# Weight parts made by one instruction a loaded chunk instead of two

## The chip, the cores and the metric

The kernel runs on one core of a Trainium2 chip. The metric is the device time of one execution in microseconds; the lower the better. Five engines work side by side, each through its own queue in order: TensorE (PE in the profile; its weight loads are listed as PEld) multiplies matrices, VectorE (DVE) and ScalarE (ACT) work elementwise, GpSimd (POOL) does the same more slowly, and SyncE (SP) issues the loads.

## The reference, cut to what matters

A decoder trunk of two layers with 256 tokens and a width of 2048, all in float32: layer 0 mixes tokens by the RWKV-7 recurrence, layer 1 by causal differential attention, and each is followed by a gated MLP with a causal depthwise convolution. Nearly all arithmetic is products of the activations with weights out of DRAM.

```python
def reference(x, ...):
    for i in range(DEPTH):                      # DEPTH = 2
        if i % 2 == 0:
            h, v_first = rwkv7_mix(x, ...)      # r, k, v = xr @ w_rkv[0], ...; scan over tokens; (y * g) @ w_o
        else:
            h = diff_attn_mix(x, ...)           # q, k, v = x @ w_qkv; softmax - lam * softmax; o @ w_o
        x = layer_norm(ALPHA * x + h, ...)
        x = layer_norm(ALPHA * x + conv_glu(x, ...), ...)   # (u * gelu(conv(g))) @ w_down, width 5504
    return x
```

## The kernel before

Activations lie with features on the partitions, in 16 tiles of 128 features ("k-tiles") by 256 tokens. A float32 product is made of products of two parts: an operand is split into `hi`, its rounding to the float32r type, and `lo`, the rest. For a weight block and one k-tile TensorE multiplies `hi` with both parts of the activations, which lie side by side (512 columns, line 225), and `lo` with the first part (256 columns, line 226). In the narrow form (lines 221 to 223) there are three matmuls of 256 columns in place of these two.

The weights' parts are made while the kernel runs, in `chunk`. A load (line 204) brings a chunk of up to `WCH = 4` k-tiles, 128 x 512 numbers, into a `raw` tile. Then, for each `HCH = 2` k-tiles, ScalarE makes `hi` by a cast (line 210), and VectorE makes `lo = raw - hi` (line 213). POOL takes over some of the subtractions: every third in the front, every fourth in the recurrence (`pool_every`), and those of the very first chunks. A `hi` or `lo` tile holds 128 x 256 numbers, a "half". Some chunks are shorter: two k-tiles for some pieces of the output projection of layer 0 and for two fifths of the pieces of `Ahead`, three at the end of each block of the MLP's second product, which has 43 k-tiles.

Tiles come from pools with a fixed number of buffers: `raw`, `hi` and `lo` have (3, 4, 4) in the first pool, which is there throughout (`PACE["w0"]`), and in those that single stages add; (6, 6, 6) in the one of the front (`PACE["vw"]`). Chunks take the open pools in turn. In the recurrence only the first pool is open. When the instructions are written, a scheduler orders them per engine by priority, by when a tile is free and by estimated durations; on the chip each engine's order is then fixed, and the waits between engines are by semaphores.

The stages, in order of time:

- the front (to about 160 us): `mix` makes the inputs of the six projections from the tokens and their shift, on VectorE and POOL, each split into its parts (lines 767, 191, 192), while the value projection and three small ones run (`lead`, `dense_pair`)
- the recurrence (to about 660 us): `pipeline` runs four steps side by side for groups of two feature tiles, `chain`, `lanes`, `front` and `products`, at set paces. `products` are the projections for k and r, in the narrow form; the others are many small matmuls with VectorE and ScalarE work between them. Towards the end `early` begins the output projection
- the rest of the output projection, the norm, and the first MLP. `Ahead` begins the first products behind a norm before the norm is known (lines 890 to 892)
- the two products of the first MLP (`glu`), the attention, the second MLP, the last norm. During the first MLP's second product a table of biases is written to DRAM and read back (`bias_table`, lines 590 and 593), in the queue of the weight loads

Of the kernel before, what the change touches and what calls it, by code (L numbers as in the profile page):

```python
# [32 lines left out]
HCH = 2  # L33
PACE = dict(chain=37.24, front=19.56, lanes=19.55, products=40.92, pool=4, pool0=3, chain0=0, front0=0,
            lanes0=0, early0=0, products0=0, wc='PVVA', ek='AA', ez='VA', ec='AVAA', ey='V', el='V', w0=(3, 4,
            4), lb=1, early=46.23, vw=(6, 6, 6), vp=2, ep='V', eg='A', lg=2, lr=2, la=4, ah=10, ao=12, ah0=0.05)
# [89 lines left out]
class Trunk:  # L126
    def __init__(self, ctx, tc, a):
# [13 lines left out]
        # ahead of each tile's parts: a norm's weights and biases, first their second parts  # L141
# [7 lines left out]
    def weight_pools(self, ctx, name, bufs=(3, 4, 4)):  # L149
        w = tuple(ctx.enter_context(self.tc.tile_pool(name=f"{n}{name}", bufs=b))  # L150
                  for n, b in zip(("raw", "hi", "lo"), bufs))
        self.wp.append(w)
        ctx.callback(self.wp.remove, w)
# [32 lines left out]
    def split(self, src, dst, lo=None):  # L186
        """dst[..., :n] and dst[..., n:] become the two parts of src."""
# [6 lines left out]
    def weights(self, src, n, pool=False):  # L194
        """src: [P, n*128] in DRAM; the parts of it, chunk by chunk."""
        for k in range(0, n, WCH):
            self.nr += 1
            yield from self.chunk(src, k, min(WCH, n - k), self.wp[(self.nr - 1) % len(self.wp)], pool and k == 0)
# [17 lines left out]
    def mm3(self, ps, hi, lo, i, xs, first, last, narrow=False):  # L216
        """ps[:, :T] += hi.xh ; ps[:, T:] += hi.xl + lo.xh, or all of it in ps[:, :T]"""
# [10 lines left out]
    def dense_steps(self, src, n, xs, evac, group=1, k0=0, step=4, pool=False, narrow=False,  # L228
                    ramp=0):
        """src: list of DRAM blocks [P, n*128], for k-tiles k0...; evac(index, psum). Yields every few k-tiles."""  # L230
        for g in range(0, len(src), group):
# [4 lines left out]
            while done < n:  # L236
                if done < ramp:
                    # the first parts of a k-tile for all blocks before its second parts
# [25 lines left out]
    def dense_pair(self, src, n, xs, evac, step=4):  # L264
        """Two blocks, each summed in half a bank; evac(psum)."""
# [15 lines left out]
    def token_steps(self, src, xs, evac):  # L281
        """src: [P, KT*T] in DRAM, T columns a k-tile; evac(psum), with tokens on partitions: [P, T/P * T]."""
        nc = self.nc
        ps = self.psum()
        for k, _, hi, lo in self.weights(src, KT * T // P):
            k = k * P // T
            for b in range(T // P):
                o = ps[:, b * T:(b + 1) * T]
                xh, xl = (xs[:, k, a + b * P:a + (b + 1) * P] for a in (0, T))
                # the bank's first product marks all of it as not written  # L290
                nc.tensor.matmul(o, lhsT=xh, rhs=hi, start=k == 0 and b == 0, stop=False)  # L291
                nc.tensor.matmul(o, lhsT=xh, rhs=lo, start=False, stop=False)  # L292
                nc.tensor.matmul(o, lhsT=xl, rhs=hi, start=False, stop=k == KT - 1 and b == T // P - 1)  # L293
            if k % 2:
                yield
# [19 lines left out]
    def rsqrt(self, v, out, n, pool):  # L315
        """out = v ** -0.5 (v > 0): a first value by ln and exp, and one step of Newton's."""
# [9 lines left out]
    def ln_begin(self, ahead=None, share=False):  # L326
        """ahead: the products to follow. share: every other tile is summed on TensorE."""
# [14 lines left out]
    def ln_colsum(self, tiles, stop=False):  # L342
        for n, (st, t) in enumerate(zip(self.ln_st, tiles)):
            # the bank's first product marks all of it as not written
# [27 lines left out]
    def ln_add(self, j, ps, part=None, narrow=False, last=False):  # L372
        """part: ALPHA * x and a first part of the sum; x in self.X without it. narrow: the sum is in ps[:, :T]."""
# [38 lines left out]
    def ln_stats(self):  # L412
        """ln_dm: the mean of what X holds; ln_rs: one over its deviation."""
# [15 lines left out]
    def ln_apply(self, i, h):  # L429
        """A step for each tile, that brings it to X and S0."""  # L430
# [56 lines left out]
    def lead(self, feed, group, *args, ramp=0, ahead=4):  # L487
        """The products of a first group of tiles, with feed making their k-tiles in S0 a chunk ahead."""
# [76 lines left out]
    def up_blocks(self, i):  # L565
        """By tiles of the hidden layer: gate, value."""
        return [self.a["ff_up"][i][(FT if q == 0 else 0) + j] for j in range(FT) for q in range(2)]

# [7 lines left out]
    def bias_table(self):  # L576
        """By distance, then by query and key; a yield where a load has to come back."""
        nc, tc = self.nc, self.tc
        with tc.tile_pool(name="bt", bufs=1) as bp, tc.tile_pool(name="bd", bufs=1, space=bass.MemoryType.DRAM) as dp:
# [8 lines left out]
            # a row for each query, read one further to the right with each  # L588
# [224 lines left out]
    def lora(self, pool, mids, g, i, evac):  # L813
        """evac(psum): the tiles of group g."""
# [31 lines left out]
class Ahead:  # L846
    """The first products of a layer, while the norm before it ends: rs ((x - m) g) W + b W, with x g W - m g W
    for (x - m) g W."""
# [25 lines left out]
    def fetch(self, wp=None):  # L874
        """The parts of the next piece of a block's weights."""
# [58 lines left out]
def _together(*todo):  # L934
    """Runs generators side by side, each at the pace of its number of steps, from a starting point on."""
# [18 lines left out]
class Groups:  # L954
    """The state recurrence for GT feature tiles (2 heads each) at a time, in chunks of C tokens."""
# [9 lines left out]
    def open(self):  # L965
# [22 lines left out]
        # blocks of 16 x 16 on the diagonals, DBL apart  # L988
# [21 lines left out]
    def early(self, n):  # L1010
        """The last projection's first k-tiles, once z's first tiles stand, into the tiles of X that are free."""
# [48 lines left out]
    def front(self, g):  # L1060
# [15 lines left out]
        # kk  # L1076
# [8 lines left out]
        # decay, cumulated in each chunk  # L1085
# [20 lines left out]
        # k <- k (1 + (a - 1) k_a) ; a <- kk a  # L1106
# [13 lines left out]
        # in-chunk products, one head in each half of the rows  # L1120
# [12 lines left out]
        # the columns of a, by units of 64 x 64, to DRAM  # L1133
# [8 lines left out]
        # bonus  # L1142
# [287 lines left out]
```

## Time and profile before

| | |
|---|---|
| time of the runs, us | 2612.49, 2617.95, 2630.53 (median 2617.95) |
| span of the profiled execution, us | 2630.5 |
| its own time, us | 2630.53 |
| TensorE busy | 2524.3 us, 96% |
| VectorE busy | 2067.1 us, 79% |
| ScalarE busy | 1642.4 us, 62% |
| POOL busy | 379.8 us, 14% |
| mean granted TensorE clock | 0.979 of full speed |

The profiled execution is the slowest of the three runs; its span and its own time agree. A busy share is a mean over the whole span, and the stages differ, so the table of stretches below tells more. Matmuls overlap, and a mean time of one matmul is longer than the step from one to the next. The time of an instruction in a group's row is its own; instructions that follow each other without a pause overlap as well.

### The profile page before, as it was taken

What the parts mean: (1) busy time and instruction counts of PE and PEld (TensorE: products, weight loads), DVE (VectorE), ACT (ScalarE), POOL (GpSimd) and SP (SyncE); (2) the same over time, 40 slices, a digit from 0 to 9 for tenths busy, and PEclk for the clock granted to TensorE, in tenths of its full rate; (3) what the DMA queues carried; (4) which work ended last, traced back from release to release, by engine and by line L of the source; (5) the groups of instructions that cost most, each with busy time, mean ns of one, the idle gap of its engine ahead of it and who ended that gap; (6) DMA issues with size and microseconds to landing.
All of it is one profiled execution on the core that took longest, in us unless ns stands there. A gap on an engine that the chain in (4) does not pass through costs nothing.

```text
span 2630.5 us, 54371 instructions
## 1 busy us (share of the span) xinstructions
PE 2524.3 (96%) x17374; PEld 2220.6 (84%) x17374; DVE 2067.1 (79%) x5108; ACT 1642.4 (62%) x4287; POOL 379.8 (14%) x457
## 2 busy tenths in 40 slices
PE   7999999999899999998899999999999999999997
PEld 6888888877788888887788999998888888888886
DVE  8977888885898777775677887778897777777776
ACT  5766455553566666664566676666676666666664
POOL 4343333331220000000111200002300000000112
PEclk9999999998999999999899999999999999999998
DMA  5544333343446555555666455555465555556664
GB/s 187 173 126 122 88 96 101 101 108 91 134 151 199 190 190 190 188 190 145 191 189 191 147 177 176 169 173 184 143 201 189 188 188 188 188 187 185 190 189 129
DMA packets 285160, 429.60 MB, mean 163 GB/s; under 512 B 69064, under 2 KB 91592, under 8 KB 284872
## 3 DMA queue, kind: packets, MB, share of 16 engines
q1 hardware_dynamic: 284872, 426.12, 53.4%
q8 instruction: 136, 2.23, 0.3%
q14 instruction: 152, 1.25, 0.2%
HBM read 419.45 MB, written 6.56 MB: 162 GB/s over the span
## 4 chain that ended last, share of the span: by engine, by line
PE 86%; DVE 7%; DMA 3%; issue 2%; ACT 1%; POOL 1%; SPq 0%; DVEq 0%; ACTq 0%; POOLq 0%
PE psd L225 41%; PE psd L226 21%; PE psd L221 3%; PE psd L223 3%; PE psd L222 3%; DVE lo L213 2%; PE pss L1127 1%; DMA raw<-in_ff_down 1%; PE psd L293 1%; PE psd L291 1%; PE psd L292 1%; DVE mx L767 1%; PE psd L891 1%; PE psd L892 1%; PE psd L890 1%
## 5 line engine op out<-in xcount | busy, mean ns | idle before, releaser
L210 ACT CAST hi<-raw 128x256 fp32r<-128x256 f32 (+1 forms) x3128 | 1229.3, 404 | 730.2 <-PE psd L225 470.8
L213 DVE TENSOR_TENSOR lo<-raw,hi 128x256 fp32r<-128x256 f32 (+1 forms) x2984 | 1291.9, 444 | 423.6 <-ACT hi L210 388.0
L225 PE MATMUL psd<-S,hi 128*128 128x512 f32 x3004 | 1058.6, 396 | 0.1
L226 PE MATMUL psd<-S,lo 128*128 128x256 f32 x3004 | 842.8, 281 | 3.4 <-DVE lo L213 3.2
L225 PEld LDWEIGHTS psd<-S,hi 128*128 128x128 f32 x3004 | 567.0, 189 | 132.6 <-ACT hi L210 1.1
L226 PEld LDWEIGHTS psd<-S,lo 128*128 128x128 f32 x3004 | 566.6, 189 | 5.0 <-DVE lo L213 3.7
L225 PE MATMUL psd<-hs,hi 128*128 128x512 f32 x1290 | 452.9, 395 | 22.7 <-ACT hi L210 22.7
L226 PE MATMUL psd<-hs,lo 128*128 128x256 f32 x1290 | 362.4, 281 | 0.7 <-DVE lo L213 0.6
L225 PEld LDWEIGHTS psd<-hs,hi 128*128 128x128 f32 x1290 | 242.7, 188 | 79.1 <-ACT hi L210 23.4
L226 PEld LDWEIGHTS psd<-hs,lo 128*128 128x128 f32 x1290 | 244.1, 189 | 1.6 <-DVE lo L213 1.5
L363 POOL COPY ln_acc<-X 128x256 f32<-128x256 f32 x4 | 2.1, 526 | 1257.4 <-DVE X L397 1257.4
L213 POOL TENSOR_TENSOR lo<-raw,hi 128x256 fp32r<-128x256 f32 x144 | 121.8, 852 | 330.2 <-ACT hi L210 253.4
L223 PE MATMUL psd<-S,lo 128*128 128x256 f32 x480 | 139.4, 290 | 15.6 <-DVE lo L213 10.0
L221 PE MATMUL psd<-S,hi 128*128 128x256 f32 x480 | 141.2, 294 | 1.5 <-ACT hi L210 1.5
L222 PE MATMUL psd<-S,hi 128*128 128x256 f32 x480 | 136.0, 283 | 0.0
L225 PE MATMUL psd<-S1r,hi 128*128 128x512 f32 x276 | 108.9, 425 | 1.3 <-DVE S1r L192 0.7
L223 PEld LDWEIGHTS psd<-S,lo 128*128 128x128 f32 x480 | 90.9, 189 | 22.4 <-DVE lo L213 14.7
L370 POOL TENSOR_TENSOR ln_acc<-ln_acc,X 128x256 f32<-128x256 f32 x49 | 40.2, 820 | 402.1 <-DVE X L409 388.6
L221 PEld LDWEIGHTS psd<-S,hi 128*128 128x128 f32 x480 | 91.1, 190 | 5.6 <-ACT hi L210 1.9
L222 PEld LDWEIGHTS psd<-S,hi 128*128 128x128 f32 x480 | 91.1, 190 | 1.7 <-issue 1.5
L221 PE MATMUL psd<-S1r,hi 128*128 128x256 f32 x284 | 87.7, 309 | 0.0
L891 PE MATMUL psd<-S,lo 128*128 128x258 f32 x256 | 77.2, 301 | 9.8 <-DVE lo L213 9.8
(295 smaller groups left out, 3921.5 us busy)
## 6 DMA issues: line engine op xcount, KB each, us to landing
raw<-in_ff_up SPq DMA_DIRECT2D x676, 256.0 KB, 3.4
raw<-in_ff_down SPq DMA_DIRECT2D x320, 256.0 KB, 2.9
raw<-in_rkv SPq DMA_DIRECT2D x192, 256.0 KB, 3.4
raw<-in_da_qk SPq DMA_DIRECT2D x122, 256.0 KB, 3.3
raw<-in_da_v SPq DMA_DIRECT2D x64, 256.0 KB, 3.0
raw<-in_da_o SPq DMA_DIRECT2D x64, 256.0 KB, 3.5
raw<-in_rw_o SPq DMA_DIRECT2D x50, 256.0 KB, 3.3
raw<-in_ff_down SPq DMA_DIRECT2D x32, 192.0 KB, 2.5
```

Source lines behind the costliest of these rows:

```text
L210: nc.scalar.copy(out=hi[:, :s * P], in_=r)
L213: eng.tensor_tensor(out=lo[:, :s * P], in0=r, in1=hi[:, :s * P].bitcast(F32), op=ALU.subtract)
L221: nc.tensor.matmul(ps[:, :T], lhsT=hi, rhs=xs[:, :T], start=first, stop=False)
L222: nc.tensor.matmul(ps[:, :T], lhsT=hi, rhs=xs[:, T:], start=False, stop=False)
L223: nc.tensor.matmul(ps[:, :T], lhsT=lo, rhs=xs[:, :T], start=False, stop=last)
L225: nc.tensor.matmul(ps, lhsT=hi, rhs=xs, start=first, stop=False)
L226: nc.tensor.matmul(ps[:, T:], lhsT=lo, rhs=xs[:, :T], start=False, stop=last)
L291: nc.tensor.matmul(o, lhsT=xh, rhs=hi, start=k == 0 and b == 0, stop=False)
L292: nc.tensor.matmul(o, lhsT=xh, rhs=lo, start=False, stop=False)
L293: nc.tensor.matmul(o, lhsT=xl, rhs=hi, start=False, stop=k == KT - 1 and b == T // P - 1)
L370: nc.gpsimd.tensor_tensor(out=self.ln_acc[:, hs], in0=self.ln_acc[:, hs], in1=t, op=ALU.add)
L891: nc.tensor.matmul(ps[:, 2:4 + T], lhsT=lo[:, w], rhs=x[:, 2:4 + T], start=False, stop=False)
```

## The change

`HCH` becomes 4, so that one cast and one subtraction make the parts of a whole chunk, 128 x 512 numbers. `hi` and `lo` tiles are twice as wide, and the pools hold half as many: (3, 2, 2) and, in the front, (6, 3, 3). Tiles for chunks of two k-tiles are as wide and half filled. POOL takes every third or fourth instruction as before. `token_steps`, which had one k-tile of 256 columns a tile, now steps through the two of a tile. The ramp of the first products (`lead` with `ramp=2`) covers four k-tiles where it covered two, since it goes by whole tiles. The other lines of the diff take comments out.

```diff
-HCH = 2
+HCH = 4
...
-            lanes0=0, early0=0, products0=0, wc='PVVA', ek='AA', ez='VA', ec='AVAA', ey='V', el='V', w0=(3, 4,
-            4), lb=1, early=46.23, vw=(6, 6, 6), vp=2, ep='V', eg='A', lg=2, lr=2, la=4, ah=10, ao=12, ah0=0.05)
+            lanes0=0, early0=0, products0=0, wc='PVVA', ek='AA', ez='VA', ec='AVAA', ey='V', el='V', w0=(3, 2, 2), lb=1, early=46.23, vw=(6, 3, 3), vp=2, ep='V', eg='A', lg=2, lr=2, la=4, ah=10, ao=12, ah0=0.05)
...
-    def weight_pools(self, ctx, name, bufs=(3, 4, 4)):
+    def weight_pools(self, ctx, name, bufs=(3, 2, 2)):
...
-        for k, _, hi, lo in self.weights(src, KT * T // P):
-            k = k * P // T
-            for b in range(T // P):
-                o = ps[:, b * T:(b + 1) * T]
-                xh, xl = (xs[:, k, a + b * P:a + (b + 1) * P] for a in (0, T))
...
-                nc.tensor.matmul(o, lhsT=xh, rhs=hi, start=k == 0 and b == 0, stop=False)
-                nc.tensor.matmul(o, lhsT=xh, rhs=lo, start=False, stop=False)
-                nc.tensor.matmul(o, lhsT=xl, rhs=hi, start=False, stop=k == KT - 1 and b == T // P - 1)
-            if k % 2:
-                yield
+        for k0, s, hi, lo in self.weights(src, KT * T // P):
+            for i in range(s * P // T):
+                k = k0 * P // T + i
+                wh, wl = (w[:, i * T:(i + 1) * T] for w in (hi, lo))
+                for b in range(T // P):
+                    o = ps[:, b * T:(b + 1) * T]
+                    xh, xl = (xs[:, k, a + b * P:a + (b + 1) * P] for a in (0, T))
...
+                    nc.tensor.matmul(o, lhsT=xh, rhs=wh, start=k == 0 and b == 0, stop=False)
+                    nc.tensor.matmul(o, lhsT=xh, rhs=wl, start=False, stop=False)
+                    nc.tensor.matmul(o, lhsT=xl, rhs=wh, start=False, stop=k == KT - 1 and b == T // P - 1)
+                if k % 2:
+                    yield
```

## Rows read from the trace of the kernel before

**Rows 1.** The table of stretches: start and end in us and the length, then for each engine its busy time and number of instructions, the granted TensorE clock, and the loads' share and rate. The last of its stretches is the whole span.

```profile
core 0: us, PE busy (x) PEld busy (x) DVE busy (x) ACT busy (x) POOL busy (x), PEclk, DMA share, GB/s
20.00:160.00 140.00, 127.24 (x936) 118.85 (x936) 136.89 (x305) 96.47 (x281) 54.95 (x64) 1.00 0.51 158
160.00:660.00 500.00, 478.05 (x4959) 401.03 (x4958) 390.14 (x929) 256.96 (x594) 155.69 (x190) 0.95 0.38 102
660.00:800.00 140.00, 129.92 (x802) 115.45 (x801) 127.09 (x312) 91.97 (x258) 38.16 (x45) 0.95 0.47 148
800.00:1230.00 430.00, 430.00 (x2470) 375.93 (x2469) 337.82 (x886) 293.29 (x767) 0.00 (x0) 1.00 0.60 190
1450.00:1550.00 100.00, 95.83 (x697) 91.33 (x696) 81.18 (x204) 66.66 (x188) 19.80 (x23) 0.97 0.53 163
...
1930.00:2610.00 680.00, 680.00 (x3924) 596.01 (x3924) 519.22 (x1320) 444.82 (x1159) 24.43 (x30) 1.00 0.60 186
0.00:2630.50 2630.50, 2524.32 (x17374) 2220.63 (x17374) 2067.13 (x5108) 1642.43 (x4287) 379.76 (x457) 0.98 0.54 163
```

**Rows 2.** The timeline of TensorE inside the first MLP's first product: start, duration, engine, line, operation, operands. The two matmuls begin one k-tile apart.

```profile
1000.02 0.39 PE L225 MATMUL psd<-S,hi 128*128 128x512 f32 x1
...
1000.37 0.39 PE L225 MATMUL psd<-S,hi 128*128 128x512 f32 x1
```

**Rows 3.** The groups by line of the stretch 800 to 1230 us: busy us and mean ns of one, then the engine's idle time before them and what ended it. VectorE's subtractions and ScalarE's casts.

```profile
L213 DVE TENSOR_TENSOR lo<-raw,hi 128x256 fp32r<-128x256 f32 x621 | 262.6, 424 | 88.1 <-ACT hi L210 80.1 <-PE psd L226 1.8
L210 ACT CAST hi<-raw 128x256 fp32r<-128x256 f32 x618 | 249.5, 405 | 120.6 <-PE psd L225 109.2 <-PE psd L226 2.1 <-ACT hi L210 0.2
```

**Rows 4.** The waits of TensorE over the whole span, longest first: who waited for whom, us in total, times, longest.

```profile
PE psd L225 <- ACT hi L210: 23.1, 3, 22.7
PE psd L223 <- DVE lo L213: 11.3, 16, 1.5
```

**Rows 5.** The timeline of the queue of loads around the hole: the raw loads behind the bias table's write, and the table's read back.

```profile
1226.62 18.83 SPq L204 DMA_DIRECT2D raw<-in_ff_down  x3
1259.95 0.38 SPq L593 DMA_DIRECT2D B<-dtab  x1
```

**Rows 6.** The groups by line and shape over the whole span: VectorE, ScalarE and POOL on parts of 256 columns, and the nearest instructions over 512.

```profile
L213 DVE TENSOR_TENSOR lo<-raw,hi 128x256 fp32r<-128x256 f32 x2952 | 1282.7, 445 | 418.6 <-ACT hi L210 383.0 <-PE psd L226 10.6 <-PE psd L225 3.3
L210 ACT CAST hi<-raw 128x256 fp32r<-128x256 f32 x3096 | 1219.9, 405 | 721.2 <-PE psd L225 462.4 <-PE psd L222 109.6 <-PE psd L293 26.9
...
L213 POOL TENSOR_TENSOR lo<-raw,hi 128x256 fp32r<-128x256 f32 x144 | 121.8, 852 | 330.2 <-ACT hi L210 253.4 <-PE psd L226 33.5 <-PE psd L223 19.8
...
L1143 POOL TENSOR_TENSOR r<-r,k 128x512 f32<-128x512 f32 x8 | 11.1, 1382 | 16.5 <-DVE AR L1118 16.5
...
L1348 POOL TENSOR_TENSOR bon<-bon,o_rs 128x512 f32<-128x512 f32 x8 | 10.3, 1288 | 8.2 <-ACT o_rs L1045 7.9
...
L192 DVE TENSOR_TENSOR S1r<-X,S1r 128x512 fp32r<-128x512 f32 x8 | 6.7, 845 | 0.1
...
L192 DVE TENSOR_TENSOR S1a<-on,S1a 128x512 fp32r<-128x512 f32 x8 | 5.5, 692 | 0.5
...
L191 ACT CAST S1a<-on 128x512 fp32r<-128x512 f32 x8 | 5.0, 620 | 0.1
```

**Rows 7.** The timeline just behind the hole, ScalarE's casts and VectorE's subtractions, six each without a pause.

```profile
1260.67 1.89 ACT L210 CAST hi<-raw 128x256 fp32r<-128x256 f32 x6 [22.03 <-DMA raw<-in_ff_down]
...
1261.11 1.97 DVE L213 TENSOR_TENSOR lo<-raw,hi 128x256 fp32r<-128x256 f32 x6 [22.09 <-ACT hi L210]
```

**Rows 8.** First the subtractions on VectorE from 0 to 160 us, by line and shape; then the table of stretches for the subtractions alone (VectorE busy, POOL busy, with their numbers).

```profile
L213 DVE TENSOR_TENSOR lo<-raw,hi 128x256 fp32r<-128x256 f32 x117 | 53.1, 480 | 0.4 <-ACT hi L210 0.4
...
20.00:160.00 140.00, 53.11 (x117) 52.93 (x58) 1.00 0.51 158
160.00:660.00 500.00, 116.47 (x230) 60.35 (x77) 0.95 0.38 102
660.00:800.00 140.00, 66.60 (x149) 4.24 (x5) 0.95 0.47 148
```

**Rows 9.** The timeline of TensorE in the first products, with the idle time before the instruction and what ended it.

```profile
13.55 0.79 PE L249 MATMUL psd<-S,hi 128*128 128x256 f32 x2 [0.72 <-DVE S L192]
```

**Rows 10.** The waits from 160 to 660 us: ScalarE's for tiles of the first part, and TensorE's for parts.

```profile
ACT hi L210 <- PE psd L222: 92.1, 129, 2.2
...
ACT hi L210 <- PE psd L225: 33.1, 35, 3.5
...
PE psd L223 <- DVE lo L213: 4.1, 5, 1.0
PE psd L223 <- POOL lo L213: 3.2, 2, 1.6
...
PE psd L221 <- ACT hi L210: 1.5, 2, 0.7
```

**Rows 11.** The timeline of one burst of products in the recurrence: TensorE's first and last matmul of it and the next burst's first, then ScalarE's first cast into a tile that came back.

```profile
340.76 0.39 PE L221 MATMUL psd<-S1r,hi 128*128 128x256 f32 x1
...
343.62 0.28 PE L223 MATMUL psd<-S1r,lo 128*128 128x256 f32 x1
...
345.51 0.39 PE L221 MATMUL psd<-S1r,hi 128*128 128x256 f32 x1
...
341.65 0.41 ACT L210 CAST hi<-raw 128x256 fp32r<-128x256 f32 x1 [0.42 <-PE psd L222]
```

## The prediction, made before the changed kernel was built

> **What bounds the kernel now.** The first view to read is the table of stretches [rows 1]. TensorE is busy for 2524.3 of 2630.5 us (the line of the whole span), and the table shows how unevenly the rest lies. From 800 to 1230 us it is busy for 430.00 of 430, and from 1930 to 2610 for 680.00 of 680: these long runs are the gated MLPs. The steps between matmuls confirm that TensorE alone sets the pace there: one k-tile (512 columns, then 256) begins 0.35 us after the one before, whatever else goes on [rows 2]. VectorE and ScalarE make the parts in the same stretch and are ahead: ScalarE's casts stand still for 109.2 us because TensorE hasn't given a part tile back [rows 3]. In such a stretch no cheaper cast moves the end.
>
> So what the change can move lies in the rest, and the waits of TensorE say how much [rows 4]. The largest one, 22.7 us, is a hole in the loads at 1238 to 1261 us and has nothing to do with the parts [rows 5]. What remains lies in the start and the first mixer (0 to 800 us) and in the starts of the later layers. Three regimes have to be told apart. From 20 to 160 us VectorE is busy for 136.89 of 140 us and TensorE for 127.24: VectorE is the bound, with TensorE's free 12.8 us as the most that can be won. From 160 to 660 us TensorE is busy for 478.1 of 500, VectorE for 390 [rows 1]. From 660 to 800 VectorE is again the fuller one in its queue, 127.1 of 140, TensorE 129.9, since both wait for each other through the norm.
>
> **What one instruction costs.** An instruction over 256 columns takes 445 ns on VectorE, 405 on ScalarE, 852 on POOL; the nearest ones over 512 columns with the same operands and types take 692 (in attention, POOL still) to 845 ns (in the recurrence, POOL at work), 620 ns, and on POOL 1288 to 1382 ns [rows 6]. That looks like a saving of 45 to 198 ns a chunk on VectorE, 190 on ScalarE and 320 to 420 on POOL. Instructions in a full queue overlap, though: six in a row take 1.97 us on VectorE and 1.89 on ScalarE, so 0.33 and 0.32 each [rows 7], 0.10 below the lone ones. In a full queue a chunk therefore costs 0.66 us today, and 0.692 - 0.096 = 0.60 afterwards: 0.06 saved.
>
> **Part by part.** *Steady stretches (800 to 1230, 1262 to 1450, 1550 to 1880, 1930 to 2610 us).* No time is removed from the path. Two pools alternate by chunk, so four chunks fit before and after. When TensorE gives a chunk's tile back, three chunks of 4 x 0.35 = 1.39 us stand ahead of its next use, 4.2 us; the new tile needs 0.62 + 0.69 = 1.31 us and what stands in VectorE's queue. Today it is seven halves, 4.85 us, against 0.85. Cover remains: 0 us. If it were gone, each chunk would pay up to 1.31 us.
>
> *The front, 20 to 160 us.* VectorE makes 117 halves in 53.1 us there, 0.454 each, 0.908 a chunk [rows 8]. Two such become one instruction. Its price lies between 0.692 and 0.845; POOL is at work here for 55 of 140 us [rows 1], so I take the row beside POOL, 0.845, less the 0.026 by which a mean of 0.480 is shortened to 0.454 in this queue [rows 8]: 0.82. Saved: 58 x 0.09 = 5 us, bounds 58 x 0.06 = 4 and 58 x 0.22 = 13. VectorE is the bound, so all of it comes off the time: -5.
>
> *The first chunk.* TensorE has to wait for a cast of 0.62 in place of 0.41 us, and the second part comes from POOL in 1.3 in place of 0.9. At 13.55 us TensorE still waits for the first mixed inputs anyway [rows 9], so of these 0.6 us I count 0.5, bounds 0 and 1.2 (two blocks start in turn on POOL).
>
> *The recurrence, 160 to 660 us.* Only the first pool is open here (the other is closed after the front), so there are two chunk tiles of each part in place of four halves. ScalarE's casts wait 125.2 us for TensorE to give a tile back: this pool is always full [rows 10]. TensorE works in bursts. From 340.76 to 343.62 us it runs through eight k-tiles, all that the pool holds, in steps of 0.36 us, and the next burst starts at 345.51; the first half is refilled from 341.65 us on, while the burst runs [rows 11]. Afterwards the first tile comes back only after four k-tiles, at 342.2. Cast 0.62 and subtraction 0.82 make it ready at 343.7, the second one (free at 343.6) by 345.1 with an idle VectorE. The next burst at 345.51 finds both. Were it to come at once, it would find neither; a chunk of a dense stream turns in (1.44 + 0.62 + 0.82 + 0.06) / 2 = 1.47 us against 1.44, with POOL, which takes every fourth, in (1.44 + 0.62 + 1.38 + 0.06) / 2 = 1.75. There are 307 halves, so 153 chunks [rows 8], and products fill 153 x 1.44 = 220 of 500 us. Without bursts that touch the price is 0. With every chunk late by 0.1 (the mean of three at 0.03 and one at 0.31) and half an instruction ahead of it on VectorE, 0.15, it is 153 x 0.25 = 38 us. TensorE's longest waits for parts sum to 8.8 us here today [rows 10]; I take a near doubling, +8, nearer to 0 since most bursts stand apart like the one shown. Against it VectorE is relieved of 115 x 0.19 = 22 us (two halves at 0.506 each [rows 8] against one instruction at 0.82), but it isn't full (390 of 500), so this shortens only waits on other results; -2 (bounds 0 and -8, all waits on parts gone). Net +6.
>
> *The norms, 660 to 800 us, and the later starts (1450 to 1550, 1880 to 1930).* VectorE makes 149 halves at 0.447 here [rows 8]. The 14 output tiles with two k-tiles left and 12 of the 30 pieces of the first MLP's early products have 256 columns, and stay as they are in number and width; some 64 chunks save 0.09 each, 6 us of VectorE, of which I count half, -3 (bounds 0 and -13). Each later start has 18 full pieces of 30, so 1.6 us of VectorE, and I count -1 each. The 256-column pieces now fill half of a tile, so half as many are held: +1.
>
> *Loads.* The raw tiles, the queue of loads and its order by chunk stay. Raw tiles come back with the chunk's one subtraction. The hole stays, but the number of raw loads issued between the table's write and its read back, three today [rows 5], can differ by one or two, 1.4 us each: 0, bounds -3 and +3.
>
> Sum: 0.5 - 5 + 6 - 3 - 2 + 1 = -2.5 us. The profiled execution is itself the slowest of the three runs (2630.53 us, no more than its span), 0.5% above the median of 2617.95, so the difference is set against the median: 2617.95 - 2.5 = 2615 us.
>
> The Trainium skill has a rule on each side. Its page "Perfetto Trace Analysis", section "Optimizing Scalar/DVE Operations", says that grouping into larger operations helps where the engine is saturated, and that where the engine isn't and still causes bubbles on others, instructions should be broken up. This trace has both states, 136.9 of 140 us in the front and 390 of 500 in the recurrence. By the first half alone the sum would be 2618 - 5 - 3 - 2 = 2608 us; what the second half would make of it stands as the first rival.
>
> **Rivals.** *A starved pool (slower).* In the recurrence TensorE meets each chunk late. For it: that pool is always full, a tile now comes back half as often, and the subtraction stands behind longer work in order on VectorE. Against it: the pause of 1.9 us between the bursts shown. It decides from the point where a chunk's next use comes less than 0.62 + 0.82 us, and VectorE's queue, after the tile is free. It gives 2618 + 38 - 8 = 2648. This is what the second half of the Trainium skill's rule, cited above, would make of it.
>
> *VectorE's relief comes through in full (faster).* Front -13, recurrence -8, norms -13 with the later starts at -4, nothing starved: 2618 - 38 = 2580; with half of it, 2599. For it: VectorE is full in the front and beside the norms. Against it: the overlap [rows 7], and TensorE at 91 to 96% there.
>
> *The change saves nothing.* The halves overlap already; a chunk costs 0.66 against 0.60. Then 2618 stays, apart from the recurrence.
>
> **How the numbers follow.** Runs of this kernel lie between 2612 and 2631 us, so under 1% (26 us) is about what can't be told from no change. Little or no change (the sum, and savings of nothing): 0.71, on its own 2597 to 2638. Starved pool to over 2644: 0.18. Relief to below 2592: 0.11. The range takes in the upper end of the starved pool with the first chunk and the hole, 2655, and the relief down to 2588; what lies outside is under 0.2.
>
> **What the profile would show.** Casts and subtractions halve in number (1564 or so), at about 0.62 and 0.69 to 0.85 us. In 800 to 1230 us TensorE stays at 430 of 430 with the step of 0.35. The front, up to TensorE's first full stretch, ends some 5 us sooner. In the recurrence TensorE's waits on parts grow from 8.8 to about 17 us; at over 30 the starved pool is right. The prediction is wrong if the order of work on the engines comes out differently around the new sizes, so that bursts lie closer, or if the hole at 1238 us widens or closes.

## The result, and the profile after

The changed kernel takes 2627.73 us (median of 18 runs, 2624.40 to 2633.71), the kernel before, run beside it, 2619.85 (18 runs, 2612.49 to 2630.53). The ratio is 1.0027, 95% interval 1.0017 to 1.0037: 8 us slower, inside the range, but on the other side of the forecast of 2615. The profiled execution has a span of 2628.5 us and a time of its own of 2630.25.

The table of stretches of the changed kernel, columns as in [rows 1]:

```profile
core 0: us, PE busy (x) PEld busy (x) DVE busy (x) ACT busy (x) POOL busy (x), PEclk, DMA share, GB/s
20.00:160.00 140.00, 128.44 (x956) 121.00 (x956) 129.69 (x247) 88.13 (x194) 47.86 (x36) 0.97 0.53 166
160.00:660.00 500.00, 471.04 (x4999) 394.04 (x4999) 388.55 (x838) 241.37 (x457) 153.60 (x153) 0.99 0.39 104
660.00:800.00 140.00, 126.58 (x780) 111.56 (x779) 118.92 (x244) 85.46 (x192) 35.25 (x41) 0.98 0.49 152
800.00:1230.00 430.00, 430.00 (x2469) 375.94 (x2469) 302.85 (x565) 241.33 (x454) 0.00 (x0) 1.00 0.60 186
1930.00:2610.00 680.00, 679.35 (x3917) 594.90 (x3915) 458.61 (x825) 361.99 (x670) 28.63 (x30) 1.00 0.61 185
0.00:2628.50 2628.50, 2507.62 (x17378) 2203.05 (x17378) 1911.80 (x3646) 1409.52 (x2755) 376.96 (x387) 0.99 0.55 163
```

VectorE and ScalarE are relieved as meant: over the whole span VectorE is busy for 1911.80 us in place of 2067.13, ScalarE for 1409.52 in place of 1642.43 [rows 1]. Their groups by line and shape (lines are one lower than before):

```profile
L212 DVE TENSOR_TENSOR lo<-raw,hi 128x512 fp32r<-128x512 f32 x1432 | 1021.2, 717 | 529.2 <-ACT hi L209 525.0
L209 ACT CAST hi<-raw 128x512 fp32r<-128x512 f32 x1500 | 925.3, 620 | 873.7 <-PE psd L224 519.1 <-PE psd L221 132.7 <-DVE lo L212 64.4
L212 POOL TENSOR_TENSOR lo<-raw,hi 128x512 fp32r<-128x512 f32 x68 | 98.9, 1460 | 241.9 <-ACT hi L209 186.5 <-DMA raw<-in_rkv 22.0 <-DVE S1r L191 13.7
```

A subtraction of 512 columns takes 0.717 us on VectorE, a cast 0.620, inside what was foretold; POOL's 1.460 is above the 1.288 to 1.382 that it was put at. TensorE's waits over the whole span, the lines that answer to [rows 4]:

```profile
PE psd L224 <- ACT hi L209: 24.3, 3, 23.0
PE psd L222 <- DVE lo L212: 13.1, 16, 2.0
PE psd L892 <- DVE lo L212: 12.6, 13, 1.9
PE psd L222 <- POOL lo L212: 9.8, 3, 5.0
```

The last two of these in the kernel before, under its own line numbers:

```profile
PE psd L891 <- DVE lo L213: 9.8, 8, 1.5
PE psd L223 <- POOL lo L213: 5.2, 5, 1.6
```

In the narrow form (line 222) TensorE now waits three times for POOL, up to 5 us (at most 1.6 before), and behind a norm (line 892) thirteen times where it had waited eight times. Which of these waits set the time is a question for the experiments.

**Clock first, then stages.** Two executions of one kernel differ, so the kernel before was profiled three times. In the profile of the prediction TensorE ran at half its clock (1.2 GHz) for some 24 us in the recurrence; in the third one (before_b) it did not. The stretches around it, first in the profile of the prediction:

```profile
620.00:630.00 10.00, 8.89 (x195) 7.01 (x194) 8.73 (x19) 5.38 (x13) 2.73 (x4) 0.87 0.48 137
630.00:650.00 20.00, 20.00 (x126) 14.84 (x126) 6.74 (x20) 3.60 (x10) 1.45 (x2) 0.50 0.11 34
```

and in before_b:

```profile
620.00:630.00 10.00, 9.55 (x235) 7.68 (x234) 8.73 (x21) 5.88 (x16) 3.37 (x4) 1.00 0.53 154
630.00:650.00 20.00, 19.73 (x169) 14.68 (x169) 12.52 (x37) 5.50 (x14) 2.20 (x3) 1.00 0.22 69
```

In both TensorE stood for a moment (busy 8.89 and 9.55 of 10 us, a stop of 1.11 and one of 0.45 us); in the first it then got the granted clock of 0.50 and did 126 matmuls in 20 us, not 169. Before_b is thus the nearest profile to compare with, 2617.6 us long against 2628.5. It still has more time at half the clock than the changed kernel: by the clock records 37.5 us against 30.7 up to the first norm and 54.4 against 42.1 behind it, so the losses below are, if anything, too small. From the timelines, split at the last column sum of the first norm:

| us | before_b | after | difference |
|---|---|---|---|
| start to the first chain | 167.5 | 166.4 | -1.1 |
| first chain to the first norm's last column sum | 550.6 | 554.5 | +4.0 |
| from there to the end of the span | 1899.5 | 1907.5 | +8.0 |

The other two profiles of before have 1901.0 and 1899.5 in the last line, a second one of after 1907.0. So most of the loss lies behind the first norm, where the prediction had looked for a gain of 2 and a cost of 1. By stages there: to the end of the first MLP's first product +1.6, its second product with the hole +3.0, attention's first products and values +1.5, the rest of attention -0.3, the third norm and the second MLP's first product +2.4, the second MLP's second product +0.1 (the stages end with the last matmul; the few us behind it make up the rest).

### The profile page after: what moved, and what is told of

The parts are those of the page before. It is cut to its first block, busy times and chain, and to the rows that moved or that the text cites. A ratio compares the mean times of both kernels' runs of the same rounds, so it can differ in the third digit from the quotient of the medians.

```text
span 2628.5 us, 48623 instructions
## 1 busy us (share of the span) xinstructions
PE 2507.6 (95%) x17378; PEld 2203.1 (84%) x17378; DVE 1911.8 (73%) x3646; ACT 1409.5 (54%) x2755; POOL 377.0 (14%) x387
## 4 chain that ended last, share of the span: by engine, by line
PE 82%; DVE 10%; DMA 3%; issue 2%; ACT 2%; POOL 1%; SPq 0%; DVEq 0%; ACTq 0%; POOLq 0%
PE psd L224 41%; PE psd L225 21%; PE psd L220 3%; PE psd L222 3%; DVE lo L212 3%; PE psd L221 3%; DMA raw<-in_ff_down 1%; PE pss L1128 1%; PE psd L293 1%; PE psd L294 1%; PE psd L292 1%; DVE mx L768 1%; ACT hi L209 1%; DMA raw<-in_rkv 1%; PE rp L1299 1%
## 5 line engine op out<-in xcount | busy, mean ns | idle before, releaser
L212 DVE TENSOR_TENSOR lo<-raw,hi 128x512 fp32r<-128x512 f32 (+2 forms) x1522 | 1063.4, 703 | 576.7 <-ACT hi L209 572.3
L209 ACT CAST hi<-raw 128x512 fp32r<-128x512 f32 (+2 forms) x1596 | 966.3, 609 | 944.2 <-PE psd L224 557.1
L212 POOL TENSOR_TENSOR lo<-raw,hi 128x512 fp32r<-128x512 f32 (+1 forms) x74 | 104.1, 1412 | 274.5 <-ACT hi L209 219.1
```

The lines of the kernel that those rows point to most:

```text
L209: nc.scalar.copy(out=hi[:, :s * P], in_=r)
L212: eng.tensor_tensor(out=lo[:, :s * P], in0=r, in1=hi[:, :s * P].bitcast(F32), op=ALU.subtract)
```

## The experiments

**The kernels themselves again.**

> The kernel before, once more, for a profile of an execution nearer to its median: the profiled one was the slowest of its runs (2630.5 us, granted clock 0.979). If the 8 us of the change are lost in the work itself, this execution should take about 2618 us and pass the stage boundaries earlier than the changed kernel from 620 us on: the stretch 620 to 700 us, at a clock of 0.7 in the first profile, about 8 us shorter, the rest unchanged within 1 us. If that stretch is not shorter, the loss sits elsewhere.

> The changed kernel unaltered, for a comparison on the same chip. Theory (the loss is spread over the later starts and the hole, and the early stages gain nothing at an equal granted clock): 2625 to 2630 us, 8 us above the kernel before, mean granted clock 0.985 to 0.987 in every execution while that of the kernel before varies from 0.977 to 0.987. Rival (the difference is of the chip used, not of the change): within 3 us of the kernel before.

> The kernel before unaltered, for one more profile of it. Theory (its stages are as long in every execution, apart from stretches at half the granted clock): from the end of the first norm to the end 1896 to 1898 us, from the first norm on as in the two earlier profiles within 1 us a stage; the time falls by about 0.4 us for each us less at half the clock, so about 2617 us in an execution at 0.986. Rival (the stages themselves differ between executions): other lengths at equal clock.

e0_before: 2620.26 us, ratio 0.9989 (0.9971 to 1.0008); its profiled execution, 2626.50 us, has the 24 us at half the clock as well, so it could not settle what it was run for. after_again: 2627.39 against 2622.14 on the same chip, 1.0022 (1.0007 to 1.0038). before_b: a single time of 2619.36. The stages do repeat within 1 us apart from the clock. The mean granted clock of the kernel before varies between executions from 0.977 to 0.987: in 119 executions the median is 2631 us at 0.979 and less (14 of them) and 2618 at 0.984 and more (45). The changed kernel lies between 0.982 and 0.988 (not between 0.985 and 0.987, as expected), and takes 2627.5 at 0.984 and more. At an equal clock it loses some 9.5 us; its steadier clock hides a part of that.

**One part alone, from the changed kernel.** wide_tiles keeps the whole tiles and fills each by two halves of instructions; pool_half leaves VectorE whole chunks, but where POOL's turn comes, in the chunks of the kernel before, POOL makes 256 columns and VectorE the other 256; roomy has three whole tiles where there were two (two still for `lo` in the first pool). The words behind `#` are labels.

```diff
+        for k in range(0, m, 2):                        # wide_tiles, one hi and lo tile a chunk
+            c = slice(k * P, (k + s) * P)
+            nc.scalar.copy(out=hi[:, c], in_=raw[:, c])
...
+        if all(e is nc.vector for e in engs):           # pool_half
+            cuts = [(0, m, nc.vector)]
+        else:
+            cuts = [(2 * i, min(2 * i + 2, m), e) for i, e in enumerate(engs)]
...
-    def weight_pools(self, ctx, name, bufs=(3, 2, 2)):
+    def weight_pools(self, ctx, name, bufs=(3, 3, 3)):  # roomy, with w0=(3, 3, 2)
```

> Part tiles of 512 columns, half as many, as in the changed kernel, but each made by two casts and two subtractions of 256 columns as before. Starved pool (a tile comes back only after four k-tiles): this is as slow as the changed kernel or slower, 2627 to 2635 us, since the front's relief is gone as well. Long instructions (a first product waits for 512 columns, a subtraction on POOL takes 1.46 us): this is back at the kernel before, 2617 to 2623 us, with TensorE's waits for parts at 34 us, not 47.

> The changed kernel with POOL's share as it was before: POOL makes the second half of a chunk (256 columns), VectorE the first half, in the same chunks as before; all other casts and subtractions stay at 512. If the long subtractions on POOL cost the time (TensorE waited 9.8 us for them in the recurrence, 4.95 and 4.38 us at once), this takes 2616 to 2620 us and these two waits are gone. Starved pool: no difference, 2627 us. Front's relief stays in both, 2.5 us.

> The changed kernel with one more tile in the pools that have room: three first-part tiles in the first pool (three raw, three hi, two lo) and three of each part in the pools of the later stages. Starved pool: waits for a free tile go and the recurrence is 8 us shorter or more, 2612 to 2620 us. Long instructions: the time stays at 2625 to 2630 us, since what is late is the making and not the tile.

Against 2623.0 for the kernel before on that chip: wide_tiles 2622.42, ratio 1.0001 (0.9986 to 1.0016), pool_half 2624.31, 1.0012 (0.9995 to 1.0029), roomy 2621.57, 0.9997 (0.9981 to 1.0013). Each takes back some 3 to 6 us. wide_tiles lies where long instructions were to put it (2617 to 2623); the other two lie between the ranges of their theories. Most of the gain comes ahead of the first norm's end, which is at 714.7 to 715.2 us where the changed kernel has 721.0. Behind it they have 1906.5, 1904.8 and 1903.9 us against 1907.5. So no single one of width, POOL or room explains the 8 us there; room takes back most, 3.6.

What POOL costs shows in the changed kernel's timeline (start, duration, operation), first POOL, then TensorE:

```profile
221.52 4.12 POOL L1108 TENSOR_TENSOR wa<-kk,wa 128x512 f32<-128x512 f32 x1 [0.95 <-DVE t L1105]
225.72 1.73 POOL L1116 TENSOR_TENSOR KB<-wa 128x256 f32<-128x256 f32 x2
227.41 1.26 POOL L212 TENSOR_TENSOR lo<-raw,hi 128x512 fp32r<-128x512 f32 x1
...
228.73 0.58 PE L222 MATMUL psd<-S,lo 128*128 128x256 f32 x1 [4.38 <-POOL lo L212]
```

The chunk's one subtraction stands behind 5.85 us of POOL's own work, and TensorE has nothing else to do for 4.38 us. The subtraction itself is the smaller part of it: POOL's own product has become longer. The same product at the same step in before_b:

```profile
222.29 2.66 POOL L1107 TENSOR_TENSOR wa<-kk,wa 128x512 f32<-128x512 f32 x1 [1.69 <-DVE t L1104]
```

It takes 2.66 us in wide_tiles too, where all subtractions are halves, 4.12 in roomy, where all are whole, and 2.28 in pool_half. What VectorE does beside it is the likely cause; which instruction of VectorE's it is wasn't shown. Nor do these waits set the time alone. TensorE's waits on POOL in the narrow form from 160 to 660 us, first in pool_half, then in roomy:

```profile
PE psd L227 <- POOL lo L217: 2.7, 2, 1.3
...
PE psd L222 <- POOL lo L212: 8.1, 2, 4.2
```

In pool_half the long ones are gone, in roomy they are not, and both come to the first norm's end equally early.

**Before and after the first norm, and more half tiles.** wide_first has the change in layer 0's mixer and its norm alone, wide_later behind them alone (the first pool is joined there by second `hi` and `lo` pools of the other width, 8 KB a partition); more_halves is the kernel before with `w0=(3, 6, 4)` and (3, 6, 6) in the stages' pools.

> The change in layer 0's mixer and its norm alone (to about 750 us); from the first MLP on the parts are made by halves into half tiles. Theory (the loss lies behind the first norm): as fast as the kernel before at a high granted clock or a little faster, 2615 to 2620 us. Rival (the starved pool of the prediction, the loss lies in the recurrence): 2625 to 2630, as the changed kernel.

> The other way round: halves in layer 0's mixer and its norm, whole chunks from the first MLP on. Theory (the loss lies behind the first norm): 2625 to 2630 us, some 7 to 8 above the kernel before, the granted clock varying as it does there. Rival (the loss lies in the recurrence): as the kernel before.

> The kernel before with halves throughout, but room for six half tiles of each part where it had four (in the first pool for the first part alone). Theory (how many parts are held decides, not the width of an instruction): faster than the kernel before by 3 to 8 us, as the roomy kernel was 6 us faster than the changed one. Rival (room doesn't matter where the tiles come back by halves): within 2 us of the kernel before.

Against 2622.14: wide_first 2630.60, ratio 1.0024 (1.0010 to 1.0038), wide_later 2634.04, 1.0050 (1.0031 to 1.0069), more_halves 2641.64, 1.0074 (1.0054 to 1.0094). Both theories miss on the first two, and the reason is a cost of the experiment, in the stretch of the first MLP, where TensorE never waits. First before_b, then wide_first:

```profile
800.00:1190.00 390.00, 390.00 (x2244) 341.69 (x2243) 307.24 (x806) 268.62 (x701) 0.00 (x0) 1.00 0.59 190
800.00:1190.00 390.00, 390.00 (x2222) 340.48 (x2221) 305.32 (x798) 265.94 (x695) 0.00 (x0) 1.00 0.58 188
```

With the same halves and the full clock, 22 matmuls fewer fit: each begins 1% later, which is 4 us in this product alone; wide_later has the same 2222. The extra pools move all later tiles in memory. These two kernels can't be read by their time. More_halves misses both its theories and loses its 19 us elsewhere, with 2244 matmuls in this stretch: it has more room and nothing taken away, and why it is slower wasn't traced; another order of the instructions is the likely reason.

**The pieces of two k-tiles.** Behind a norm, `Ahead` takes a block's 16 k-tiles in pieces of 4, 4, 4, 2 and 2. In half tiles the last two fill one each; in whole tiles they fill a half. ahead_halves casts and subtracts these early pieces by halves into whole tiles; full_pieces makes the last two one piece; full_again is the same kernel, timed; before_full is the kernel before with the same edit.

```diff
-        self.items = [(k, m, b) for k, m in ((0, 4), (4, 4), (8, 4), (12, 2), (14, 2)) for b in range(len(src))]
+        self.items = [(k, m, b) for k, m in ((0, 4), (4, 4), (8, 4), (12, 4)) for b in range(len(src))]
```

> The change, but the pieces of the early products behind a norm are cast and subtracted by halves, still into whole tiles. Theory (each start behind a norm is later because its first parts come from longer instructions): the stretch from the last column sum to the last early product is again 42.6 to 43.0 us in layer 0's second norm and 41.8 us in layer 1's, against 42.8 in the changed kernel, and the values' stage and the second MLP's first product lose the 1.1 and 1.3 us that they got longer; in all 3 to 4 us off, 2623 to 2625. Rival (the loss comes from whole tiles that come back late): no stage shorter than in the changed kernel.

> The change, with early products in 24 pieces of four k-tiles in place of 18 of four and 12 of two, so that no tile is half filled. Theory (half-filled tiles hold too few parts at the end of the early products): the stalls behind them, 0.4 to 1.4 us each at the start of the values' stage and of both MLPs, go; 3 to 4 us off, 2623 to 2625. Rival (whole-chunk instructions cause them): they stay, 2627 or more, since a block now ends later.

> The change with 24 early pieces of four k-tiles, timed. Theory (half-filled tiles cost the 7 to 8 us behind the first norm): 2620 to 2622 us, 6 below the changed kernel; from the first norm's end to the end 1897 to 1898 us again. Rival (the one profile was a chance): 2626 to 2628.

> The kernel before with 24 early pieces of four k-tiles; its half tiles are full either way. Theory (the gain in the changed kernel comes from tiles that are no longer half filled): no gain here, within 3 us of the kernel before. Rival (pieces of four k-tiles are better in themselves): 5 to 8 us below it, 2612 to 2615.

ahead_halves: 2628.49, and 1907.2 us behind the first norm: nothing gained, the width of the instructions isn't it. full_pieces: 2622.21 in its one execution; full_again 2622.41, ratio 0.9995 (0.9980 to 1.0010) to the kernel before. Behind the first norm they have 1900.0 and 1899.8 us: 7 to 8 us come back, in the stages that had lost them (1.4, 1.6, 2.8 and 1.6 us in full_again, in the order of the list above without attention's rest). The second of these, at the hole, is the clock's, as the next section shows; against it full_again has 3.4 us each at half the clock in the first and third, which the changed kernel has not. The median time falls by 5 us. before_full: 2623.27, 1.0002 (0.9984 to 1.0020), and 1901.5 us there: no gain. So pieces of two k-tiles cost the changed kernel some 5 to 7 us, and the kernel before nothing.

How it looks, at the end of the early products of layer 0's second norm. The changed kernel, ScalarE and TensorE:

```profile
1510.80 0.41 ACT L209 CAST hi<-raw 128x256 fp32r<-128x256 f32 x1 [0.86 <-PE psd L893]
1511.52 0.41 ACT L209 CAST hi<-raw 128x256 fp32r<-128x256 f32 x1 [0.31 <-PE pss L893]
...
1518.96 0.14 ACT L919 COPY lw<-pss 128x4 f32<-128x4 f32 x1
...
1519.11 0.49 PE L651 MATMUL pss<-qk 128*128 128x128 f32 x2 [1.09 <-ACT lw L919]
```

full_again, ScalarE at the same place:

```profile
1510.20 0.61 ACT L209 CAST hi<-raw 128x512 fp32r<-128x512 f32 x1
1510.76 0.62 ACT L209 CAST hi<-raw 128x512 fp32r<-128x512 f32 x1
```

In the changed kernel ScalarE's casts of half-filled tiles stand still until TensorE gives a tile back (0.86 and 0.31 us), with the small copies and evictions queued behind them, and for one of these copies TensorE later waits 1.09 us. With full pieces none of the three waits is there. That the first two lead to the third is read from the order of the queue, not shown by itself.

**Both cures, and where the rest lies.** halves_roomy is wide_tiles with roomy's tiles; full_roomy is full_pieces with them; full_roomy_pool adds pool_half's way of making `lo`. proj_halves and proj_room change the tiles of the output projection's own pool alone (four half tiles, or three whole ones).

> Whole tiles filled by two halves of instructions, with room for three whole tiles of each part (two of the second part in the first pool). Theory (the width of an instruction and the number of tiles each cost some us): the gains of the two single kernels over the changed one, 5 and 6 us, add up to 9 or more, 2616 to 2619. Rival (how the order of the instructions comes out decides, as with more half tiles, which cost 19 us): anywhere from 2617 to 2640, with the stages' lengths unlike those of either kernel.

> The change with 24 early pieces of four k-tiles and three tiles where there were two (two still for the second part in the first pool). Theory (two separate places of the same cause: the output projection's pieces of two k-tiles, helped by more tiles, and the early products): first norm's end at 714 to 716 us, from there 1897, 2613 to 2616 us, below the kernel before at any clock. Rival (another order decides): 2618 or more.

> As the kernel with full pieces and more tiles, and POOL's subtractions as before of 256 columns in the same chunks, VectorE making the other half. Theory (POOL's 1.5 us instructions cost the recurrence some 5 us): last chain's start at 610 to 612 us in place of 615 to 617, and so 2608 to 2612 us. Rival (another order decides): not below the kernel with POOL on whole chunks.

> The change, with half tiles (four of each part) and instructions over 256 columns in the output projection's own pool alone, which takes every other chunk of it. Theory (half-filled tiles in the output projection): from the last chain's start to the first norm's end 99 to 103 us where the changed kernel has 105.5 and the kernel before 98.3 at full clock; the stages behind as in the changed kernel. Rival (the loss there lies in the first pool or in the norm itself): 105 us.

> The change, with three whole tiles of each part in place of two in the output projection's own pool alone. Theory (too few tiles for pieces of two k-tiles): 98 to 102 us from the last chain's start to the first norm's end, as with three in all pools (97.6), the stages behind as in the changed kernel. Rival (the first pool decides): 105 us.

halves_roomy: 2624.85 against 2620.62, ratio 1.0013 (1.0000 to 1.0026): the two gains of 5 and 6 us do not add up, as the rival said. full_roomy: 2612.23 against 2621.82, 0.9954 (0.9939 to 0.9969). full_roomy_pool: 2609.69, 0.9947 (0.9927 to 0.9967). Both beat the kernel before, with 1893.6 and 1892.5 us behind the first norm where that has 1899.5. The two cannot be told apart by their intervals, and POOL's part is missed: the last chain starts at 619.0 us, not at 610 to 612, though half the granted clock from about 252 us on for some 14 us stands in that profile. Not tried: the kernel before with full pieces and as much more room, so the gain over it is shown for these kernels and not for its cause. proj_halves and proj_room: 2628.24 and 2632.03 in one execution each, 103.4 and 104.4 us from the last chain to the norm's last column sum, outside both theories' ranges (to 103 and to 102) and 1 to 2 us below the changed kernel's 105.5, where roomy has 97.6. So the output projection's own pool is not where roomy gains its 8 us there; the first pool or the others are, which wasn't tried apart.

## Why the prediction was wrong, step by step

The sum was -2.5 us; between before_b and the changed kernel's profile it is +10.9. Three terms were far off: the front by 3 to 4 us, the later starts with their half-filled tiles by 6, the hole by 3. In the front, and at least in part in the later starts, the same step failed: it was taken for granted that TensorE gives whole tiles back early enough for ScalarE's next casts. The hole was put at nothing, and what the change added there were two longer waits and 3.4 us at half the clock.

- **Steady stretches, 0:** right but for their first microseconds. From 800 to 1230 us TensorE is busy for 430.00 of 430 with 2469 matmuls against 2470 [rows 1]. From 1930 to 2610 it has 679.35.
- **The front, -5:** the relief is there, the time isn't. VectorE's busy time in 20 to 160 us falls from 137.70 in before_b to 129.69, but the first chain starts only 1.1 us sooner. The step "VectorE is the bound, so all of it comes off" failed. (The granted clock there is 0.97, and 0.98 in before_b; the first chunk's +0.5 lies in the same stretch.) VectorE's own waits there grow from 2.0 to 10.3 us, first of all these (from 20 to 160 us: who waited for whom, total, times, longest):

```profile
DVE lo L212 <- ACT hi L209: 5.4, 2, 3.1
DVE S L191 <- ACT S L190: 3.8, 3, 2.1
```

  It waits for ScalarE's casts, which ended waits of 0.6 and 0.6 us in before_b. ScalarE isn't too busy (88.13 of 140 us); its casts wait for TensorE to give a tile back. That wait in the same stretch, first in before_b, then in the changed kernel, and one case of it there:

```profile
ACT hi L210 <- PE psd L222: 5.4, 16, 0.7
...
ACT hi L209 <- PE psd L221: 13.9, 15, 1.9
...
80.03 0.62 ACT L209 CAST hi<-raw 128x512 fp32r<-128x512 f32 x1 [1.61 <-PE psd L221]
81.49 0.62 ACT L209 CAST hi<-raw 128x512 fp32r<-128x512 f32 x1 [0.84 <-PE psd L221]
...
82.86 0.62 ACT L209 CAST hi<-raw 128x512 fp32r<-128x512 f32 x1 [0.26 <-PE psd L221]
...
83.51 0.69 DVE L212 TENSOR_TENSOR lo<-raw,hi 128x512 fp32r<-128x512 f32 x1 [2.30 <-ACT hi L209]
```

  Three casts in turn stand for a tile, and the subtraction behind the third stands for 2.30 us. The prediction priced the return of tiles in the recurrence, but not here.
- **The recurrence, +6, and the norm, -3:** together +3 foretold, +4.0 measured, and that with less time at half the clock than in before_b. TensorE's waits for parts from 160 to 660 us were to grow from 8.8 [rows 10] to 17; they sum to 16.0 (POOL 9.8 and 1.1, VectorE 2.9 and 2.2). The kind was only half seen: more than half of it is two waits of 4 to 5 us on POOL's queue, so that the sum came near is in part luck. What the change costs there is larger than the +4.0: wide_tiles, pool_half and roomy need 546.9, 547.0 and 545.5 us for this stretch, against 554.5 in the changed kernel and 550.6 in before_b (which has 7 to 14 us more at half the clock in it than these three). The starved pool's +38 did not come. Two readings were off: at 0.447 a half a chunk saves 0.07 us beside the norm and not 0.09, and from 660 to 800 us TensorE, busy for 129.9 us, was the fuller engine and not VectorE with 127.1.
- **Later starts, -2, and half-filled tiles, +1:** the step that decided. Behind the first norm it was 8 us slower, and pieces of two k-tiles account for most of it (full_pieces against before_full: 5 to 7 us). The term was sized as a few parts less held. That is not the whole mechanism either: roomy has room for five or six such pieces, between the four of the changed kernel and the eight of before, and yet it has 308.6 us where the second norm and the values take 305.0 in before_b, 306.5 in the changed kernel and 303.7 in full_again. There (1483 to 1516 us) the casts' waits are now mostly for raw loads; ScalarE's longest wait is for the norm's work on VectorE:

```profile
ACT X L446 <- DVE X L445: 4.0, 1, 4.0
ACT hi L209 <- DMA raw<-in_da_v: 3.2, 2, 2.2
ACT hi L209 <- PE psd L893: 1.2, 1, 1.2
```

  Whether the tiles' fill acts by the return of tiles alone or by the order of the instructions that comes with it stays open.
- **The hole, 0, bounds -3 and +3:** it came at the upper bound. The hole itself is 22.97 us (22.69 in before_b), but two waits of 1.14 and 1.04 us follow it, for a cast and a subtraction, where there were 0.45 and 0.57 for two subtractions. That makes 1.4 us; the rest is the clock. Four microseconds behind these waits, first in the changed kernel, then in full_again:

```profile
1265.00:1269.00 4.00, 4.00 (x16) 3.44 (x15) 1.96 (x4) 1.24 (x2) 0.00 (x0) 0.57 0.78 225
...
1267.00:1271.00 4.00, 4.00 (x25) 3.52 (x24) 2.34 (x5) 1.86 (x3) 0.00 (x0) 1.00 0.85 264
```

  full_again has the same three stops (22.82, 1.14 and 1.04 us) at the full clock, and its stage is 1.6 us shorter.
- **The rule of the Trainium skill** (page "Perfetto Trace Analysis", section "Optimizing Scalar/DVE Operations") says that grouping can improve throughput if the engine is saturated. VectorE's busy time in the front agrees, 8 us less; the time does not follow, as the first chain came 1.1 us sooner. The same section of the Trainium skill says that breaking up instructions may let work complete sooner where an engine that isn't saturated causes bubbles on others. With that wide_tiles agrees, whose halves make it 5 us faster than the changed kernel, but not ahead_halves, where halves gained nothing.
- **The clock** was in no term. The kernel before loses a varying time to it (91.9 to 112.2 us at half the clock in its three profiles), and the change less (72.8 and 72.2).

## What to carry to other kernels

When a tile's width is doubled, list every user that brings less than a whole tile: those can pay, and matching their pieces to the tile (here 24 of four k-tiles) and one tile more turned a loss of 8 us into a gain of 9.6. An engine that is full is the bound only if whoever feeds it is ahead of it; look at what its freed time will wait for, and when the feeder gets its tiles back. Compare stages between profiles whose granted clock agrees there, and repeat the profile of the kernel before until it does.

## What the runs showed of the hardware

- Stops of TensorE of 1.11 and 1.20 us at 626 and 623 us, in two profiles of the kernel before, were followed by some 24 us at half the clock. A stop of 0.45 us at the same place in the third profile, and one of 1.09 us at 1518 us in the changed kernel, were followed by none. Over 119 executions of the kernel before the time falls by 1.8 us for each 0.001 of mean granted clock.
- The same matmuls at a granted clock of 1.00 and without any wait took 1% longer when two more pools of 8 KB together lay in memory (2222 in place of 2244 matmuls in 390 us, in wide_first and in wide_later). More memory in itself isn't it: more_halves and roomy, whose pools are larger too, keep 2244 and 2243. That the place of the operands is the cause is possible, but wasn't tried by itself.
- POOL's 512-column subtraction takes 1.46 us on average. One elementwise product of 512 columns on POOL took 4.12 us in the changed kernel, 2.66 at the same step of before_b, and 1.66 in most later steps of the changed kernel.
